# Three branches for the loads of a pass's last two heads, with smaller pieces only for the last pass

## The chip, the cores and the metric

One core of one Trainium2 chip. The time is the device time of one execution in microseconds; lower is better. The kernel before takes 1071.82 us (median of 3 runs, 1071.46 to 1071.98). The trace is one further execution with its own span, some 2 us shorter than the time.

## The reference

Softmax over rows of given scores, times v:

```python
batch, n_heads, seq, head_dim = 8, 12, 1024, 64      # scores: 8 x 12 x 1024 x 1024 fp32, v: 8 x 12 x 1024 x 64 fp32
scores_max = np.max(scores, axis=-1, keepdims=True)
attn = np.exp(scores - scores_max)
attn = attn / (np.sum(attn, axis=-1, keepdims=True) + 1e-8)
return np.matmul(attn, v)
```

There are 96 heads, each with 4 MB of scores, 256 KB of v and 256 KB of output.

## The kernel before

A loop of 24 passes handles four heads each, with one buffer per head for scores and v. A head's 1024 rows lie as 128 partitions x 8 rows ("row" below means one of these 8: 128 x 1024 scores). For each two rows ACT takes the exponential, for each row PE transposes it in eight 128x128 blocks, DVE copies the transposed row out of PSUM, and PE multiplies it with v (two rows later, `LAG`). A column of ones beside v gives the row sums; after four rows DVE divides. When the last row of head k has been transposed, the load of head k of the next pass is issued on SP's queue, which also has the stores.

```python
    def load(k, n, step=R, **cond):                     # R = 8 rows a head, AHEAD = 4 heads a pass
        queue(nc.sync.dma_start(out=v_bufs[k][:], in_=one(v_bh, n), **cond))
        for r in range(0, R, step):
            queue(nc.sync.dma_start(out=s_bufs[k][:, r : r + step, :],
                                    in_=one(sc_bh, n)[:, r : r + step, :], **cond))

    def load_next(k, n0):
        n = (n0 + (AHEAD + k)) % BH
        load(k, n, R if k < AHEAD - 1 else R // 2, cond=n0 < BH - AHEAD)   # skipped in the last pass

    def heads(n0):
        for k in range(AHEAD):
            nc.gpsimd.tensor_copy(out=vones_bufs[k][:, :, 0:D], in_=v_bufs[k][:])
            ...
            for r in range(R):
                if r % EB == 0:                         # EB = 2 rows
                    p_nat = take(p_bufs)
                    nc.scalar.activation(out=p_nat[:], in_=s_bufs[k][:, r : r + EB, :], func=EXP)
                ...                                     # eight transposes of row r into psT
                nc.vector.tensor_copy(out=pt[:], in_=psT[:])
                if r == R - 1:
                    load_next(k, n0)
                pending.append((n0 + k, r, pt, st))
                if len(pending) > LAG:                  # LAG = 2
                    finish(pending.pop(0))              # matmuls with v; after 4 rows divide; after 8 store
        while pending:
            finish(pending.pop(0))

    for k in range(AHEAD):
        load(k, k)
    with tc.For_i(0, BH, AHEAD, iteration_sync="reg_based") as n0:
        queued.clear()
        heads(n0)
```

`queue` keeps the transfers on SP in the order written. The build gives each transfer one of eight completion semaphores in turn, and each transfer waits until the earlier user of its semaphore has landed (in the trace of before the stores wait 292 us in all for loads of scores).

The softmax here doesn't subtract the row's maximum and nothing guards it: scores larger than these inputs give would overflow.

## Time and profile before

| | before |
|---|---|
| time, median of 3 | 1071.82 us |
| span of the trace | 1070.1 us |
| queue in service | 99.7% of the span |
| busiest compute engines (PE, ACT) | 70%, 69% |
| a pass at the queue's rate | 43.9 us |
| last landing of scores | about 1057.1 us |
| last write of out_sb ends | 1066.29 us |

The share of busy time says that data movement bounds the kernel; the timeline of the last pass says what follows the last landing. The prediction below shows the lines of both. A landing is read as the moment at which an engine's idle time before an instruction ends. One more view of before is needed, the busy table of three stretches of the tail (stretch, its length, then busy us and number of instructions of PE, PE's weight loads, DVE, ACT and POOL, the granted tensor clock, the DMA share and GB/s; in such short stretches the last two are rough):

```profile
1044.00:1048.00 4.00, 1.49 (x28) 1.24 (x26) 2.16 (x5) 1.66 (x1) 0.30 (x1) 1.00 1.03 432
1048.00:1052.00 4.00, 3.69 (x47) 3.70 (x48) 1.99 (x5) 4.00 (x4) 0.32 (x1) 0.59 1.04 446
1052.00:1056.00 4.00, 3.72 (x74) 3.60 (x72) 3.13 (x7) 4.00 (x3) 0.00 (x0) 0.98 0.85 351
```

PE has little to do before head 2 lands at 1046.3 (1.49 of 4 us).

### The profile page before, as it was taken

How to read it: one execution, taken by the hardware profiler on the slowest of the kernel's cores; microseconds unless marked ns; L12 is line 12 of the kernel's file. 1: busy time of each engine (PE TensorE's matmuls, PEld its weight loads, DVE VectorE, ACT ScalarE, POOL GpSimd, SP SyncE). 2: the span in 40 equal slices, each digit the busy share in tenths (PEclk: the TensorE clock that was granted, in tenths of full speed). 3: DMA queues.
4: the chain of work that ended last, by engine and by line, in shares of the span. 5: the costliest groups of instructions: out<-in, count | busy, mean ns of one | idle time of the engine just before them, and what ended most of it. 6: DMA issues, size and time to landing. Idle time of an engine off the chain costs nothing.

```text
span 1070.1 us, 31933 instructions
## 1 busy us (share of the span) xinstructions
PE 752.8 (70%) x12288; PEld 711.3 (66%) x12288; DVE 610.7 (57%) x1157; ACT 733.8 (69%) x408; POOL 60.1 (6%) x102
## 2 busy tenths in 40 slices
PE   3766768677676776677766768668676776767766
PEld 3766767577666676576765758567675676666766
DVE  2655656456565565555655656556564565655655
ACT  4767766677667776676856767677666776576865
POOL 0000000000000000000000000000000000000000
PEclk9888888778897888877887888888897788878889
DMA  9999999999999999999999999999999999999995
GB/s 401 430 410 430 430 431 425 432 436 431 431 426 425 434 427 425 431 431 430 433 427 434 420 442 430 421 433 426 429 426 434 432 431 431 429 424 440 430 420 228
DMA packets 44787, 453.05 MB, mean 423 GB/s; under 512 B 4976, under 2 KB 4976, under 8 KB 29552
## 3 DMA queue, kind: packets, MB, share of 16 engines
q1 hardware_dynamic: 44784, 453.00, 99.7%
q8 instruction: 3, 0.05, 0.0%
HBM read 445.64 MB, written 25.17 MB: 440 GB/s over the span
## 4 chain that ended last, share of the span: by engine, by line
DMA 67%; PEld 9%; PE 9%; DVE 5%; ACT 5%; SPq 2%; issue 2%; ACTq 0%
DMA s_nat<-in_scores_dram 67%; PEld L169 7%; PE psT L169 6%; DVE pt L175 5%; ACT p_nat L163 5%; PE psO L105 3%; PEld L105 3%; SPq L140 1%; SPq L143 1%; SPq L124 0%; DVE recip L116 0%; ACTq L163 0%; DVE out_sb L117 0%
## 5 line engine op out<-in xcount | busy, mean ns | idle before, releaser
L163 ACT ACTIVATE p_nat<-s_nat 128x2048 f16<-128x2048 f32 x384 | 703.0, 1902 | 159.2 <-DMA s_nat<-in_scores_dram 157.0
L175 DVE COPY pt<-psT 128x1024 f16<-128x1024 f16 x768 | 516.3, 690 | 432.3 <-PE L169 214.5
L169 PE MATMUL psT<-ident,p_nat 128*128 128x128 f16 x6144 | 569.7, 251 | 267.3 <-ACT p_nat L163 266.6
L169 PEld LDWEIGHTS <-p_nat 128*128 128x128 f16 x6144 | 492.9, 153 | 282.2 <-ACT p_nat L163 277.7
L105 PE MATMUL psO<-vones,pt 128*128 128x65 f16 x6144 | 374.8, 205 | 45.3 <-DVE pt L175 38.9
L105 PEld LDWEIGHTS <-pt 128*128 128x128 f16 x6144 | 305.2, 106 | 71.8 <-DVE pt L175 70.1
L163 ACT ACT_TABLE_LOAD x24 | 30.8, 1283 | 168.1 <-DMA s_nat<-in_scores_dram 163.2
L158 POOL CAST vones<-v_sb 128x512 f16<-128x512 f32 x96 | 59.4, 619 | 987.6 <-DMA v_sb<-in_v_dram 725.0
L117 DVE TENSOR_TENSOR out_sb<-psO,recip 128x256 f32<-128x256 f32 x192 | 81.1, 422 | 4.9
L116 DVE RECIPROCAL recip<-psO 128x4 f32<-128x4 f32 x192 | 33.5, 174 | 17.2 <-PE psO L105 17.2
L57 DVE MEMSET vones<- 128x8 f16 x4 | 0.2, 65 | 0.8 <-PEq L204 0.8
L51 DVE CAST ident<-ident 128x128 f16<-128x128 f32 x1 | 0.2, 226 | 0.3 <-POOL ident masks.py:199 0.3
masks.py:199 POOL TENSOR_SCALAR_AFFINE_SELECT ident<-ident 128x128 f32<-128x128 f32 x1 | 0.3, 294 | 0.1
masks.py:197 POOL MEMSET ident<- 128x128 f32 x1 | 0.2, 205 | 0.3 <-POOLq L204 0.3
L204 POOL MEMSET const-float32-0.0<- 128x1 f32 x1 | 0.1, 99 | 0.2 <-issue 0.2
L204 POOL MEMSET const-bfloat16-1.0<- 128x1 bf16 x1 | 0.1, 102 | 0.0
L204 POOL MEMSET const-uint8-127<- 128x1 uint8 x1 | 0.1, 102 | 0.0
L204 POOL MEMSET const-float32-1.0<- 128x1 f32 x1 | 0.1, 99 | 0.0
## 6 DMA issues: line engine op xcount, KB each, us to landing
s_nat<-in_scores_dram SPq DMA_DIRECT2D x76, 4096.0 KB, 27.1
s_nat<-in_scores_dram SPq DMA_DIRECT2D x48, 2048.0 KB
v_sb<-in_v_dram SPq DMA_DIRECT2D x100, 256.0 KB, 17.2
out_dram<-out_sb SPq DMA_DIRECT2D x96, 256.0 KB, 21.1
```

The lines of the kernel that those rows point to most:

```text
L51: nc.vector.tensor_copy(out=ident16[:], in_=ident32[:])
L57: nc.vector.memset(vo[:, :, D : D + 1], 1.0)
L105: nc.tensor.matmul(out=psO[:, g, :], lhsT=pt[:, c * P : (c + 1) * P], rhs=st["vones"][:, c, :], start=(c == 0), stop=(c == C - 1),)
L116: nc.vector.reciprocal(out=recip[:], in_=psO[:, :, D : D + 1])
L117: nc.vector.tensor_tensor(out=st["out_sb"][:, r - G + 1 : r + 1, :], in0=psO[:, :, 0:D], in1=recip[:].to_broadcast([P, G, D]), op=mybir.Al ...
L140: queue(nc.sync.dma_start(out=v_bufs[k][:], in_=one(v_bh, n), **cond))
L143: nc.sync.dma_start(out=s_bufs[k][:, r : r + step, :], in_=one(sc_bh, n)[:, r : r + step, :], **cond,)
L158: nc.gpsimd.tensor_copy(out=vones_bufs[k][:, :, 0:D], in_=v_bufs[k][:])
L163: nc.scalar.activation(out=p_nat[:], in_=s_bufs[k][:, r : r + EB, :], func=EXP)
L169: nc.tensor.transpose(out=psT[:, c * P : (c + 1) * P], in_=p_row[:, c, :], identity=ident16[:],)
L175: nc.vector.tensor_copy(out=pt[:], in_=psT[:])
L204: nc = _bacc.Bacc("TRN2", target_bir_lowering=False, num_devices=1)
```

## The change

The intent: in the last pass, work should follow closely behind the data, so the last two heads of that pass come in pieces (4,4 rows and 2,2,2,2 rows). In other passes whole heads are loaded. As the loop body is one program for all passes, this choice is a branch at the end of the pass: whole heads; or pieces for the last pass, loaded in the last but one; or nothing, in the last pass itself. Apart from that, the last two rows of each pass's last head get an exponential each.

```diff
-    def load(k, n, step=R, **cond):
+    def load(k, n, parts=(R,), **cond):
 ...
     def load_next(k, n0):
-        n = (n0 + (AHEAD + k)) % BH
-        load(k, n, R if k < AHEAD - 1 else R // 2, cond=n0 < BH - AHEAD)
+        if k < AHEAD - 2:
+            load(k, (n0 + (AHEAD + k)) % BH, cond=n0 < BH - AHEAD)
+
+    def load_last(n0):
+        before = queued[-1:]
+        def loads(parts2, parts3):
+            queued[:] = before
+            load(AHEAD - 2, (n0 + (2 * AHEAD - 2)) % BH, parts2)
+            load(AHEAD - 1, (n0 + (2 * AHEAD - 1)) % BH, parts3)
+        with tc.If(n0 < BH - 2 * AHEAD) as cmp:
+            loads((R,), (R,))
+        with cmp.Else():
+            with tc.If(n0 < BH - AHEAD):
+                loads((4, 4), (2, 2, 2, 2))
 ...
-                    nc.scalar.activation(
-                        out=p_nat[:], in_=s_bufs[k][:, r : r + EB, :], func=EXP
-                    )
+                    rows = 1 if k == AHEAD - 1 and r == R - EB else EB
+                    for g in range(0, EB, rows):
+                        nc.scalar.activation(
+                            out=p_nat[:, g : g + rows, :],
+                            in_=s_bufs[k][:, r + g : r + g + rows, :],
+                            func=EXP,
+                        )
 ...
         while pending:
             finish(pending.pop(0))
+        load_last(n0)
```

More of the change, by code (lines that the diff above doesn't have):

```diff
@@ L137, in apart @@
         )
-    def load(k, n, step=R, **cond):
+    def load(k, n, parts=(R,), **cond):
         queue(nc.sync.dma_start(out=v_bufs[k][:], in_=one(v_bh, n), **cond))
-        for r in range(0, R, step):
+        r = 0
+        for rows in parts:
             queue(
                 nc.sync.dma_start(
-                    out=s_bufs[k][:, r : r + step, :],
-                    in_=one(sc_bh, n)[:, r : r + step, :],
+                    out=s_bufs[k][:, r : r + rows, :],
+                    in_=one(sc_bh, n)[:, r : r + rows, :],
                     **cond,
@@ L148, in load @@
             )
+            r += rows
     def load_next(k, n0):
-        n = (n0 + (AHEAD + k)) % BH
-        load(k, n, R if k < AHEAD - 1 else R // 2, cond=n0 < BH - AHEAD)
+        if k < AHEAD - 2:
[11 more added lines that the diff above has]
+                loads((4, 4), (2, 2, 2, 2))
     def heads(n0):
```

## The prediction

> **What bounds the kernel now.** I read the page first: busy shares, the forty slices, the queues, the chain. Then the waits, and last the timeline of each engine over the first 100 us and the last 70 us, because the change speaks of "the last pass".
>
> The page's engine line, slices, queue share and chain:
>
> ```profile
> PE 752.8 (70%) x12288; PEld 711.3 (66%) x12288; DVE 610.7 (57%) x1157; ACT 733.8 (69%) x408; POOL 60.1 (6%) x102
> DMA  9999999999999999999999999999999999999995
> GB/s 401 430 410 430 430 431 425 432 436 431 431 426 425 434 427 425 431 431 430 433 427 434 420 442 430 421 433 426 429 426 434 432 431 431 429 424 440 430 420 228
> q1 hardware_dynamic: 44784, 453.00, 99.7%
> DMA 67%; PEld 9%; PE 9%; DVE 5%; ACT 5%; SPq 2%; issue 2%; ACTq 0%
> ```
>
> No compute engine is above 70%. The one queue that carries the data was in service for 99.7% of the span, and only the last of the forty slices is not full. So for some 1057 us of 1070 the kernel is its traffic, 453 MB, at about 430 GB/s. A head is 4096 + 256 + 256 KB; a pass of four heads is 18.87 MB, and 18.87 MB / 430 GB/s = 43.9 us.
>
> ACT at the end of the run (start, duration, what, idle before it and what ended that):
>
> ```profile
> 1002.40 14.72 ACT L163 ACTIVATE p_nat<-s_nat 128x2048 f16<-128x2048 f32 x8 [3.65 <-DMA s_nat<-in_scores_dram]
> 1024.41 1.28 ACT L163 ACT_TABLE_LOAD   x1 [7.28 <-DMA s_nat<-in_scores_dram]
> 1025.70 7.32 ACT L163 ACTIVATE p_nat<-s_nat 128x2048 f16<-128x2048 f32 x4
> 1035.41 7.32 ACT L163 ACTIVATE p_nat<-s_nat 128x2048 f16<-128x2048 f32 x4 [2.39 <-DMA s_nat<-in_scores_dram]
> 1046.34 14.71 ACT L163 ACTIVATE p_nat<-s_nat 128x2048 f16<-128x2048 f32 x8 [3.60 <-DMA s_nat<-in_scores_dram]
> ```
>
> Each idle stretch ends with a landing. 1046.34 - 1002.40 = 43.94 us: the pass is the traffic time just worked out. Landings of the last pass: heads 0, 1 and 2 at about 1024.4, 1035.4 and 1046.3. For head 2's eight rows ACT has to wait for the whole head, and from there runs through heads 2 and 3 without a gap.
>
> SP and DVE in the last 45 us:
>
> ```profile
> 1024.48 0.33 SPq L140 DMA_DIRECT2D v_sb<-in_v_dram  x1
> 1025.36 1.19 SPq L143 DMA_DIRECT2D s_nat<-in_scores_dram  x2
> 1035.43 0.36 SPq L124 DMA_DIRECT2D out_dram<-out_sb  x1
> ...
> 1052.51 0.36 SPq L124 DMA_DIRECT2D out_dram<-out_sb  x1
> 1057.35 0.07 SPq L140 DMA_DIRECT2D v_sb<-in_v_dram  x1
> ...
> 1065.87 0.42 DVE L117 TENSOR_TENSOR out_sb<-psO,recip 128x256 f32<-128x256 f32 x1
> 1066.32 0.36 SPq L124 DMA_DIRECT2D out_dram<-out_sb  x1
> ```
>
> In the built program the store at 1052.51 waits for the semaphore of head 3's first half, and the skipped v load at 1057.35 for that of the second half. So these give the last two landings: about 1052.3 and 1057.1. After 1057.1 only 13 us of tail remain: four to five rows of compute still to do, and from the last store's issue to the end 1070.1 - 1066.3 = 3.8 us. ACT started head 3's second half at 1046.34 + 6 x 1.84 = 1057.4, just when it landed: the tail is paced by compute that began at head 2's landing (16 rows), not by the last landing.
>
> [...] the slices here sit at 430, so there is nothing for the steady state to gain. [...] The trace before has a loop branch 24 times and shows no cost above the 43.94 us of traffic; whether the new branches stall, no run shows yet.
>
> **The change part by part.**
>
> 1. *Where the loads stand.* Before, SP's order in a pass is: load 0, store 0, load 1, store 1, load 2, store 2, load 3 in halves, store 3 (loads are for the next pass). After: load 0, store 0, load 1, stores 1, 2, 3, then the branch with loads 2 and 3. So loads 2 and 3 now wait for store 3, that is for head 3's whole compute. Is the queue still fed? Call T the landing of head 3. Before T, load 0 is already issued (its semaphore's earlier user, load 2 of this pass, landed at T - 11). Load 1 waits for head 3's own semaphore, issued at T + 1. Head 3's compute takes about 9.5 us after its landing (head 1: landing 1035.4, last out_sb at 1044.8), so store 3 goes at T + 10, loads 2 and 3 between T + 10 and T + 13. At that time the queue still has load 1 and three stores, full until about T + 22.5. Margin about 10 us; cost on the path 0. Likewise at the pass's end SP waits for stores to land (T + 25), while loads 2 and 3 hold the queue until T + 44.
>
> 2. *Branches.* Two compares on each engine, 24 times. Compute engines have 43.9 - 32 = 12 us of slack a pass, SP 10: hidden, cost 0. Only in the last pass, after the last store, SP additionally walks through the empty arm, waits for eight semaphores in turn, and closes: an estimate of 0.5 us on the end.
>
> 3. *Head 3 whole instead of halves.* 22 passes x 128 = 2816 packets fewer of 44787. Heads in halves land no further apart than whole ones (10.8 against 10.9 and 11.0), so worth 0.
>
> 4. *Order of stores in the tail.* Before, stores 2 and 3 of the next to last pass stand behind loads 2 and (store 3) 3; after, both stand ahead of them. 256 KB is 262144 B / 430 GB/s = 0.6 us each. So head 2 of the last pass lands 1.2 us later, head 3 0.6 us later: last landing 1057.7 instead of 1057.1.
>
> 5. *Pieces in the last pass.* Head 2's first four rows land half a head earlier than the whole: 1047.5 - 4.9 = 1042.6. ACT is free of head 1 at 1035.41 + 7.32 = 1042.7, runs them to 1046.4, and continues with rows 4 to 7 at 1047.5 to 1051.2. Head 3 in four pieces of 1 MB (2.4 us each): about 1050.5, 1052.9, 1055.3, 1057.7. Each piece needs 1.84 us on ACT, less than its 2.4 us of landing, so ACT now keeps up with the landings and the tail starts from the last piece: 1057.7.
>
> 6. *The last two rows one at a time.* One 128x1024 exponential: I take 1.0 us (half of 1.90 plus something for the fixed part). Row 7 ready at 1059.8; without the split it would be 1059.6, but row 6 can go a unit earlier. Costs 24 more ACT instructions a run, some 0.1 us a pass, hidden.
>
> The new end: 1059.8 + transposes 0.7 + DVE copy 0.69 + matmuls 0.45 + reciprocal 0.2 + multiply 0.42, with hand-overs about 0.1 = 1062.4, against 1066.29 (1065.87 + 0.42) before: 3.9 us less. Add 0.5 for the empty arm[...]. Sum: 0 in 23 passes, -3.2 us in the tail. 1071.82 - 3.2 = 1068.6 us.
>
> **The rivals.**
>
> *Queue runs dry.* If loads 2 and 3 came later than T + 22.5, every pass would show a gap. For: they move behind store 3, and the trace shows SP blocked at each pass by a few us. Against: the 10 us margin. If the branch plus its waits ate, say, 12 us, the cost would be 2 us x 23 = 46 us, slower by 4%. The waits for balance at the arm's end stand after the loads, so I hold this at 3%.
>
> [...]
>
> *PE becomes the bound of the tail.* Heads 1 to 3 then come without a pause, and the granted clock was 0.59 between 1048 and 1052 and 0.76 between 1040 and 1044 (busy table by stretches). A row costs PE, DVE about 1.0 us at best, so 16 rows from 1045 end at 1061 plus 1.3 for the last matmuls and evacuation: 1062.3, the same as the landing path. If the clock falls for longer, 1 to 2 us of the gain go: 1070.
>
> *Landing later than thought.* Three stores in a row might disturb the reads: 0.1 us a pass would be 2 us in all. Nothing before speaks for it, as a store now goes among reads at every head at 430 GB/s.
>
> **Range and chances.** Gains are bounded: even an end right at the last landing plus 3 us compute and the store cannot save more than 5.5 us, so 1066.3. Losses without a dry queue reach about +2 us. Range 1065.6 to 1072.4. Faster by over 2% (under 1050.4) would need more bandwidth: 0.01. Slower by over 2% (over 1093.3) needs the dry queue: 0.03. The rest, 0.96, within 2%.
>
> **What would show it.** The DMA row stays at 9 in all slices but the last, the queue share at 99.7% or so. The ACT timeline repeats at 43.9 us; a period of 45 or more proves me wrong in step 1. SP's timeline shows loads 2 and 3 about 10 to 13 us after head 3's landing. In the last pass ACT starts head 2 at about 1042.7, then comes in short groups that wait for landings, and its last instruction is two of 128x1024 at about 1058; the last out_sb ends at about 1062.4 and the end follows 4.3 us later. If PE shows a gapless run from 1044 with a clock well under 0.9, the third rival took part of the gain. If the last store is followed by more than 5 us, the empty arm costs more than I put down.

Cut from it: a term of 0.2 us for the tensor clock. The sum had come to -3.2 us and 1068.6 us; with the terms that stand the gain is 3.9 - 0.5 = 3.4 us. Three things that stand were estimates: that the steady state has nothing to gain; that a later place in SP's program lands later by the bytes ahead of it (the landings of before came in the order of issue, 11.0, 10.9 and 10.8 us apart); and 0.5 us for the empty arm, for which the runs below show 0.7.

## The result

The changed kernel takes 1068.99 us (median of 4 runs, 1068.56 to 1069.59), before in the same rounds 1071.9 us. The ratio is 0.9974 (95% interval 0.9957 to 0.9991). A ratio here is the mean time of one kernel's fast runs over that of the other's fast runs of the same rounds, so it is not quite the ratio of the medians. By the 2% rule the two kernels are the same; the interval leaves a gain of 0.1 to 0.4%. The span of the trace went from 1070.1 to 1066.8 us.

The slices and the queue of the changed kernel:

```profile
DMA  9999999999999999999999999999999999999996
q1 hardware_dynamic: 42048, 453.00, 99.8%
```

Nothing runs dry: the row is at 9 up to the last slice. There are 42048 packets instead of 44784 for the same 453 MB.

ACT in the last pass of the changed kernel:

```profile
1023.54 1.28 ACT L182 ACT_TABLE_LOAD   x1 [2.77 <-DMA s_nat<-in_scores_dram]
...
1034.56 7.33 ACT L182 ACTIVATE p_nat<-s_nat 128x2048 f16<-128x2048 f32 x4 [2.40 <-DMA s_nat<-in_scores_dram]
1042.07 3.72 ACT L182 ACTIVATE p_nat<-s_nat 128x2048 f16<-128x2048 f32 x2 [0.19 <-DMA s_nat<-in_scores_dram]
1046.94 7.39 ACT L182 ACTIVATE p_nat<-s_nat 128x2048 f16<-128x2048 f32 x4 [1.15 <-PE L105]
1054.85 1.91 ACT L182 ACTIVATE p_nat<-s_nat 128x2048 f16<-128x2048 f32 x1 [0.52 <-PE L105]
1057.39 2.01 ACT L182 ACTIVATE p_nat<-s_nat 128x1024 f16<-128x1024 f32 x2 [0.63 <-PE L105]
```

Where before has one block of eight activations from 1046.34, ACT now starts head 2 at 1042.07 with its first four rows, and goes in small groups with short waits. The last three waits are put down to PE. I read them as landings, the last at about 1057.3, because SP goes on at the same moments. In the last pass its skipped loads and its stores still wait for the transfer that had their semaphore before:

```profile
1046.96 0.36 SPq L124 DMA_DIRECT2D out_dram<-out_sb  x1
...
1050.00 0.07 SPq L144 DMA_DIRECT2D s_nat<-in_scores_dram  x1
1052.43 10.22 SPq L124 DMA_DIRECT2D out_dram<-out_sb  x3
```

The waits before these three are put down to loads of scores, and SP has two more such waits, which end at about 1054.8 and 1057.25. From 1050.0 on they end about 2.4 us apart, which is one piece of 1 MB, and ACT's groups at 1054.85 and 1057.39 follow the last two. The runs with other pieces below agree, as ACT's waits move with the pieces.

The last write of out_sb on DVE and the last store on SP, changed kernel:

```profile
1061.87 0.42 DVE L117 TENSOR_TENSOR out_sb<-psO,recip 128x256 f32<-128x256 f32 x1
1062.32 0.33 SPq L124 DMA_DIRECT2D out_dram<-out_sb  x1
```

So out_sb is complete at 1062.29 instead of 1066.29, 4.0 us earlier, and from the last store's issue to the end there are 1066.8 - 1062.3 = 4.5 us instead of 3.8. Together 3.3 us, the whole difference between the two spans.

The tensor clock in the same three stretches, changed kernel:

```profile
1044.00:1048.00 4.00, 3.45 (x68) 3.20 (x66) 3.36 (x7) 2.85 (x2) 0.40 (x1) 1.00 1.02 430
1048.00:1052.00 4.00, 3.50 (x69) 3.25 (x68) 3.11 (x7) 4.00 (x3) 0.21 (x1) 1.00 1.01 426
1052.00:1056.00 4.00, 3.53 (x71) 3.29 (x70) 3.25 (x7) 3.48 (x3) 0.00 (x0) 1.00 0.86 352
```

PE has no pause before head 2 any more and works at a clock of 1.00 all through; it does 69 matmuls between 1048 and 1052 where before did 47.

One ordinary pass of the changed kernel, ACT at the start of head 3 and then SP:

```profile
573.71 7.42 ACT L182 ACTIVATE p_nat<-s_nat 128x2048 f16<-128x2048 f32 x5 [3.07 <-PE psO L105]
```

```profile
575.11 11.07 SPq L124 DMA_DIRECT2D out_dram<-out_sb  x3
586.65 0.35 SPq L140 DMA_DIRECT2D v_sb<-in_v_dram  x1
587.32 0.35 SPq L144 DMA_DIRECT2D s_nat<-in_scores_dram  x1
...
588.76 0.33 SPq L144 DMA_DIRECT2D s_nat<-in_scores_dram  x1
```

With head 3's landing taken as T = 573.7, store 3 is the last of the three stores, issued at 586.18 - 0.35 = 585.8 or T + 12.1; the v load of head 2 goes at T + 12.9, the scores of heads 2 and 3 at T + 13.6 and T + 15.1. From the end of the last store's issue to the v load there are 0.47 us, and between two ordinary issues next to each other 0.32 us, so the branch itself costs SP about 0.15 us.

### The profile page after: what moved, and what is told of

It reads as the page before. It is cut to its first block, busy times and chain, and to the rows that moved or that the text cites. A ratio compares the mean times of both kernels' runs of the same rounds, so it can differ in the third digit from the quotient of the medians.

```text
span 1066.8 us, 32321 instructions
## 1 busy us (share of the span) xinstructions
PE 762.6 (71%) x12288; PEld 722.4 (68%) x12288; DVE 609.8 (57%) x1157; ACT 736.3 (69%) x432; POOL 59.9 (6%) x102
## 2 busy tenths in 40 slices
DMA packets 42051, 453.05 MB, mean 425 GB/s; under 512 B 4672, under 2 KB 4672, under 8 KB 29248
## 3 DMA queue, kind: packets, MB, share of 16 engines
q1 hardware_dynamic: 42048, 453.00, 99.8%
## 4 chain that ended last, share of the span: by engine, by line
DMA 49%; PE 20%; PEld 9%; ACT 8%; DVE 7%; issue 3%; SPq 3%; DVEq 0%; ACTq 0%
DMA s_nat<-in_scores_dram 49%; PE psT L190 13%; ACT p_nat L182 8%; PE psO L105 7%; PEld L190 6%; DVE pt L196 5%; PEld L105 3%; DVE out_sb L117 2%; SPq L140 1%; SPq L124 1%; SPq L144 1%; DVE recip L116 0%; SPq L166 0%; DVEq L196 0%; ACTq L182 0%
## 5 line engine op out<-in xcount | busy, mean ns | idle before, releaser
L182 ACT ACTIVATE p_nat<-s_nat 128x2048 f16<-128x2048 f32 (+1 forms) x408 | 705.5, 1800 | 253.5 <-DMA s_nat<-in_scores_dram 130.6
L190 PE MATMUL psT<-ident,p_nat 128*128 128x128 f16 x6144 | 583.9, 254 | 257.0 <-ACT p_nat L182 256.1
L190 PEld LDWEIGHTS <-p_nat 128*128 128x128 f16 x6144 | 501.3, 154 | 274.9 <-ACT p_nat L182 271.1
L105 PEld LDWEIGHTS <-pt 128*128 128x128 f16 x6144 | 309.0, 107 | 64.0 <-DVE pt L196 60.3
```

The source lines that it names most:

```text
L105: nc.tensor.matmul(out=psO[:, g, :], lhsT=pt[:, c * P : (c + 1) * P], rhs=st["vones"][:, c, :], start=(c == 0), stop=(c == C - 1),)
L182: nc.scalar.activation(out=p_nat[:, g : g + rows, :], in_=s_bufs[k][:, r + g : r + g + rows, :], func=EXP,)
L190: nc.tensor.transpose(out=psT[:, c * P : (c + 1) * P], in_=p_row[:, c, :], identity=ident16[:],)
```

## The experiments

The theory: the gain is made in the last pass alone, by pieces of both heads, and the branches cost nothing while the queue is full. The rivals: the gain comes from the 22 other passes (fewer packets, another order of transfers); one head's pieces are enough; the branches aren't needed; the queue is near to running dry. The results of all twelve kernels were found correct against the reference. The runs were made in three sessions on three chips; each ratio is to before in the same rounds (1071.9 to 1072.0 us in every session).

### Undoing the pieces: both heads, one head

**Both arms whole.** Edit to the changed kernel:

```diff
-                loads((4, 4), (2, 2, 2, 2))
+                loads((R,), (R,))
```

> The change with its branches and its new order, but both arms load heads 2 and 3 whole (no pieces for the last pass). Theory A (the gain is made only in the last pass, by pieces): head 2 lands whole at about 1046.8, head 3 whole at 1057.3; ACT then has 8 rows left, 7.4 us, so the last out_sb ends near 1067.8 and the span is near 1072.3, time near 1074.4, ratio to before about 1.002. Rival B (the gain comes from the passes: fewer packets, another order of loads and stores, 3 us over 22 passes): the time stays near 1069, ratio 0.997.

Measured: 1075.27 us, ratio to before 1.0028 (1.0014 to 1.0042). Span 1073.2.

**Only head 3 in pieces.**

```diff
-                loads((4, 4), (2, 2, 2, 2))
+                loads((R,), (2, 2, 2, 2))
```

> The change, but in its second arm only head 3 is in pieces (2,2,2,2), head 2 whole. Theory A': both splits are needed, since with head 2 whole ACT starts its last 16 rows at 1046.9 and they pace the end as before: last out_sb at about 1066.9, span about 1071.3, time about 1073.4, ratio 1.0012. Rival D (the last head's pieces alone make the gain): time near 1069.

Measured: 1073.38 us, ratio 1.0013 (0.9999 to 1.0027).

**Only head 2 in pieces.**

```diff
-                loads((4, 4), (2, 2, 2, 2))
+                loads((4, 4), (R,))
```

> The change, but in its second arm only head 2 is in pieces (4,4), head 3 whole. Theory A': head 3's eight rows start only at its landing, 1057.3: ACT ends at 1064.8, last out_sb at about 1067.7, span about 1072.2, time about 1074.3, ratio 1.002. Rival E (head 2's pieces alone make the gain, as it paces the end in before): time near 1069 to 1070.

Measured: 1075.97 us, ratio 1.0037 (1.0023 to 1.005).

ACT's last lines in the three runs, in this order:

```profile
1047.02 7.32 ACT L182 ACTIVATE p_nat<-s_nat 128x2048 f16<-128x2048 f32 x4 [5.05 <-DMA s_nat<-in_scores_dram]
1057.29 7.42 ACT L182 ACTIVATE p_nat<-s_nat 128x2048 f16<-128x2048 f32 x5 [2.95 <-DMA s_nat<-in_scores_dram]
```

```profile
1047.40 14.62 ACT L182 ACTIVATE p_nat<-s_nat 128x2048 f16<-128x2048 f32 x9 [5.12 <-DMA s_nat<-in_scores_dram]
```

```profile
1057.62 7.42 ACT L182 ACTIVATE p_nat<-s_nat 128x2048 f16<-128x2048 f32 x5 [6.56 <-DMA s_nat<-in_scores_dram]
```

All that the change does in the passes is in these three kernels too, and they are 4.4 to 7.0 us slower than the change (medians) and no faster than before. So the pieces of the last pass carry the gain, and both heads need them: with head 2 whole, 16 rows run in one block from its landing; with head 3 whole, eight rows stand behind the last landing. One piece without the other is worth at most 1.9 us (1075.27 to 1073.38), both together 6.3 us (1075.27 to 1068.99). The first of the three is 3.3 us slower than before. Loading head 3 whole makes 2.2 us of that (the run "Head 3 whole in before" below); about 1.1 us is left for the new order with its branch.

For the first and the third my estimate was too low, by 0.9 and 1.7 us. What I had left out is probably the tensor clock, though no run isolates it: between 1060 and 1064 it was 0.62 in the first run and 0.50 in the third, after PE's pause, and out_sb was complete 4.7 and 5.1 us after ACT's end instead of the 2.9 that I took over from the changed kernel.

### Without branches: pieces in every pass

Edit to the changed kernel:

```diff
-        if k < AHEAD - 2:
-            load(k, (n0 + (AHEAD + k)) % BH, cond=n0 < BH - AHEAD)
+        parts = ((R,), (R,), (4, 4), (2, 2, 2, 2))[k]
+        load(k, (n0 + (AHEAD + k)) % BH, parts, cond=n0 < BH - AHEAD)
 ...
-        load_last(n0)
```

> No branch at all: the order of before, with head 2 in 4,4 rows and head 3 in 2,2,2,2 in every pass, and the single-row exponentials. Theory A: the tail is as in the change or better (stores 2 and 3 of the pass before stay behind loads, the empty arm at the end is gone: 0.7 us), span about 1066.0, time about 1068, ratio about 0.9965; the passes stay at 43.9 us because eight transfers in flight still hold at least 10 us of data. Rival C (small pieces in every pass cost queue time or let it run dry, which is why the branches are there): pass period over 44.0 us, time over 1070.

Measured: 1071.09 us, ratio 0.9991 (0.9977 to 1.0005). This is what rival C said; my number was 3 us too low. The tail is as short as in the change: the last piece's exponentials start at 1060.30 and out_sb is complete at 1065.20, 4.9 us later in both. But the pass takes 44.07 us instead of 43.9 and pushes the last landing 3 us back. The queue is in service for 100.2% of the span, so it did not run dry; it moved the same bytes more slowly. That pointed at the number of packets: 54723 instead of 42051.

### What a packet costs

Two runs to test that. **Small packets in before**: each head's scores as even rows and odd rows, two transfers in 4 KB packets.

```diff
-        for r in range(0, R, step):
+        for h in range(2):
             queue(nc.sync.dma_start(
-                    out=s_bufs[k][:, r : r + step, :], in_=one(sc_bh, n)[:, r : r + step, :], **cond))
+                    out=s_bufs[k][:, h::2, :], in_=one(sc_bh, n)[:, h::2, :], **cond))
```

> The kernel of before with each head's scores loaded as even rows and odd rows (two transfers of 2 MB in 4 KB packets: 1024 packets a head instead of 128). If a packet costs 3.7 ns on its engine, as the 0.13 us a pass of the run with pieces in every pass says (12672 packets more over 16 engines took 2.9 us more), a pass of four heads costs 224 packets an engine more, 0.83 us: period 44.75 us, over the run some 19 us, and with whole heads at the end some 3 us more: time about 1094, ratio 1.021. Rival (the 0.13 us a pass came from the lanes or the order of stores, not from packets): period 43.9 to 44.1, time about 1075.

Measured: 1099.19 us, ratio 1.0256 (1.0242 to 1.027).

**Head 3 whole in before**, nothing else:

```diff
-        load(k, n, R if k < AHEAD - 1 else R // 2, cond=n0 < BH - AHEAD)
+        load(k, n, R, cond=n0 < BH - AHEAD)
```

> The kernel of before with one edit: head 3 loaded whole in every pass, no branch. Theory P (a packet costs about 5 ns on its engine: periods 43.891, 43.936, 44.066 and 44.97 us at 0, 8, 32 and 224 packets an engine and pass over whole loads): period 43.89 in the first dozen passes, last landing about 1 us earlier than before (1056.2), but head 3's 8 rows then all behind it: last out_sb at about 1068.3, time about 1074. Rival (halving costs the queue nothing, as the prediction held): period 43.94.

Measured: 1074.16 us, ratio 1.0019 (1.0006 to 1.0033), with the last landing at 1056.3 and out_sb complete at 1068.51. All three as expected.

ACT's table load opens each pass after the landing of head 0, so its start is a good clock of the passes. Twelve passes apart, for before, for before with head 3 whole, and for before with small packets:

```profile
101.78 1.28 ACT L163 ACT_TABLE_LOAD   x1 [7.25 <-DMA s_nat<-in_scores_dram]
629.01 1.28 ACT L163 ACT_TABLE_LOAD   x1 [7.26 <-DMA s_nat<-in_scores_dram]
```

```profile
101.61 1.28 ACT L163 ACT_TABLE_LOAD   x1 [3.59 <-DMA s_nat<-in_scores_dram]
628.32 1.28 ACT L163 ACT_TABLE_LOAD   x1 [3.60 <-DMA s_nat<-in_scores_dram]
```

```profile
102.79 1.28 ACT L163 ACT_TABLE_LOAD   x1 [3.90 <-DMA s_nat<-in_scores_dram]
642.42 1.28 ACT L163 ACT_TABLE_LOAD   x1 [3.88 <-DMA s_nat<-in_scores_dram]
```

| kernel | extra packets an engine and pass | a pass, us (difference / 12) | extra ns a packet |
|---|---|---|---|
| whole heads (nine kernels) | 0 | 43.891 to 43.893 | |
| before (head 3 in halves) | 144 / 16 = 9 | 43.936 | 4.9 |
| pieces in every pass | 576 / 16 = 36 | 44.066 | 4.8 |
| even and odd rows | 3648 / 16 = 228 | 44.969 | 4.7 |

The packets are the differences of the queue's counts in the traces, divided by the passes loaded. A further transfer brings its data packets (128, one a partition) and 16 of under 512 B (the pages count 4976 of these in before and 4672 in the change, for 19 transfers fewer); the expectations above counted the 128 alone, hence their 5 ns. The line is straight over a factor of 25: on the full queue a packet costs 4.7 to 4.9 ns on its engine, for scores in packets of 4 to 16 KB. It is not a cost of transfers: the last two rows of the table both have four transfers more in a pass. What the cost consists of, no run here shows. I used 3.7 ns for the small packets from a first reading of the run with pieces, and so missed its time by 5 us.

For the change this means: whole heads in 22 passes save about 0.044 x 22 = 1.0 us. In the one trace of the changed kernel little of it shows, as passes 14 to 22 of that run (counted from 0) took up to 44.0 us (43.925 on average over 21 passes, before 43.935). All seven traces of kernels with whole heads, a branch and a full queue have such late passes, of up to 44.12 us, from pass 14 at the earliest and pass 21 at the latest; over the run they cost 0.1 to 0.9 us. The two kernels with whole heads and no branch in the loop have none (43.88 to 43.91 us while they loop). So the branch, or the order of transfers that comes with it, may not be quite free; no run separates the two, and the cause stays open. The saving also cancels against an order of stores that costs an estimated 0.6 us (256 KB at 430 GB/s) at the last landing. Without the pieces it cannot outweigh a longer tail: with head 3 whole in before, the pass is shorter and the time 2.2 us longer.

### Without branches: the last two passes behind the loop

Edit to before (the single-row exponentials in the last pass too):

```diff
-    with tc.For_i(0, BH, AHEAD, iteration_sync="reg_based") as n0:
+    with tc.For_i(0, BH - 2 * AHEAD, AHEAD, iteration_sync="reg_based") as n0:
         queued.clear()
         heads(n0)
+    queued.clear()
+    heads(BH - 2 * AHEAD)      # loads the last pass in (R,), (R,), (4, 4), (2, 2, 2, 2)
+    heads(BH - AHEAD)          # loads nothing
```

> No branches: the last two passes stand behind the loop as straight code, pieces only in the last pass, order of before. Theory F (the end of the loop waits for every transfer and engine, so the queue runs empty there): heads of the last but one pass are computed only after its last landing, the queue is empty for about 10 us, time about 1078, ratio about 1.006; one slice of the DMA row at 7 or 8. Rival (the loop's end costs nothing, straight code is the better branch): tail as in the change without the empty arm, time about 1067.7, ratio 0.996.

Measured: 1090.17 us, ratio 1.0169 (1.0155 to 1.0183). ACT around the loop's end, and the queue there:

```profile
1013.58 1.28 ACT L172 ACT_TABLE_LOAD   x1 [37.99 <-PEq L229]
```

```profile
1010.00:1015.00 5.00, 0.00 (x0) 0.00 (x0) 0.00 (x0) 1.41 (x2) 1.41 (x3) 0.50 0.11 43
```

The direction was right: ACT, PE and DVE wait 37 to 38 us at the loop's end until everything has landed, and the queue then stands nearly empty (0.11). The size was three times what I put down, as I counted the empty queue alone. Behind that, the eight heads of the last two passes are computed in a row from 1013.6, 64 rows at about 1.07 us, and that, not the queue, sets the end. So here the branches have a use: they keep the last pass inside the loop.

### The single rows

Edit to the changed kernel:

```diff
-                    rows = 1 if k == AHEAD - 1 and r == R - EB else EB
+                    rows = EB
```

> The change without its single-row exponentials: rows 6 and 7 of each pass's last head in one activation again. Theory: after the last piece's landing at 1057.3 both rows are ready at 1059.3 (in the change row 6 at 1058.4, row 7 at 1059.4), so only row 6's transposes and copy shift; last out_sb ends at about 1062.7 instead of 1062.3, time about 1069.4, a difference at the noise. Rival: the split carries 1 us or more: time 1070 or more.

Measured: 1069.32 us, ratio to before 0.9974 (0.9961 to 0.9988), out_sb complete at 1063.17. Its median is 0.3 us above the change's. In its trace out_sb is complete 0.9 us later, of which 0.35 us is a later last pass (head 0's table load at 1023.89 instead of 1023.54), so the single rows are worth about half a microsecond, which the times cannot tell from nothing.

### How near the queue is to running dry

With both arms whole, one more load or all of them were put behind store 3.

```diff
-        if k < AHEAD - 2:
+        if k < AHEAD - 3:       # and load(1, ...) first in the branch; or k < 0 and load(0, ...), load(1, ...)
```

> As the run with branches and whole heads in both arms, but with head 1's load in the branch too, behind store 3. Theory M (margin is what the queue still holds when loads are issued at about 10.5 us after head 3's landing): only load 0 and three stores are left, 12.2 us, against an issue at 11 to 11.5 us plus a latency of up to 2 us, so the period is 43.9 to 45.0 us, say 44.4; time 1075 to 1100. Rival (two heads in the branch were already near the edge): period over 50 us.

> As before, with all four loads in the branch. Theory M: at head 3's landing nothing is queued but stores, loads come 10 us later, a pass takes 10 + 0.6 + 4 x 10.36 + up to 2 us of latency = 53.5 us: time about 1290, the DMA row at 8 all through. Rival (the queue isn't what feeds the pass): period under 50 us.

The latency of up to 2 us in these two was an estimate. In the trace of before the quickest load of 256 KB landed 2.7 us after its issue, and its data take 0.6 us of that at 430 GB/s.

Measured: 1143.66 us, ratio 1.068 (1.0651 to 1.071), with three heads; 1392.79 us, ratio 1.3005 (1.2979 to 1.3032), with four. Passes took 46.9 and 57.4 us on average. Both are longer than I expected, by 2.5 and 4 us, and by the same two terms. First, head 3 takes 12 us from its landing to store 3 in these kernels and in the change, not 9.5. Second, data flows about 2.5 us after an issue: with four heads, the first v load went at 518.06 and head 0's scores landed at 530.96; 4.46 MB at 430 GB/s are 10.36 us of that. With these, four heads make 12.9 + 2.5 + 4 x 10.36 = 56.8 us, measured 57.4. Three heads: the queue held load 0 and three stores, 10.36 + 1.84 = 12.2 us, and new data flows at 12.9 + 2.5 = 15.4, a gap of 3.2 us; measured 46.9 - 43.9 = 3.0.

For the change, the same sum is 15.4 us against about 22.5 us that the queue still holds: two heads in the branch leave 7 us of margin, three are too many. The rival of a dry queue falls for the change, and these runs show what it would have looked like.

### Taking the empty arm off the end

Two versions meant to beat the change. The branch moves ahead of store 3, to the last row's transposes, so that in the last pass SP has walked the empty arm before it issues the last store. The first version also cut the last head into 2,2,2,1,1:

```diff
-                loads((4, 4), (2, 2, 2, 2))
+                loads((4, 4), (2, 2, 2, 1, 1))
 ...
                 if r == R - 1:
                     load_next(k, n0)
+                    if k == AHEAD - 1:
+                        load_last(n0)
 ...
-        load_last(n0)
```

> A version meant to beat the change: the branch with loads 2 and 3 stands ahead of store 3, so that the empty arm of the last pass is walked before the last store is issued, and store 3 stays behind the last loads; the last head of the last pass comes in rows 2,2,2,1,1. Theory: last landing 0.6 us earlier than in the change (1056.7), one row less behind it, end after the last store 3.8 us instead of 4.5: span about 1065.4, time about 1067.5, ratio to before about 0.996. Rival: DVE paces the last rows or waits for the store of the pass before, and nothing is gained: time 1069.

Measured: 1080.54 us, ratio 1.008 (1.0066 to 1.0094), 13 us off. The trace of POOL and PE near the end:

```profile
1057.28 1.18 POOL L175 CAST vones<-v_sb 128x512 f16<-128x512 f32 x2 [31.23 <-DMA s_nat<-in_scores_dram]
1057.95 0.54 PE L105 MATMUL psO<-vones,pt 128*128 128x65 f16 x7 [10.99 <-POOL vones L175]
```

Head 2's v had long landed, but its cast waited 31 us, and PE waited 11 us for the cast. In the built program the second arm has nine transfers for eight semaphores: the last single row uses the one that head 2's v has, and the cast waits for that semaphore's last count. The next run keeps the place of the branch and takes the ninth transfer away:

```diff
-                loads((4, 4), (2, 2, 2, 1, 1))
+                loads((4, 4), (2, 2, 2, 2))
```

> As the version with rows 2,2,2,1,1, but with the change's own pieces 2,2,2,2, so that the second arm has eight transfers for eight semaphores. Theory (the 8.6 us lost there came from the ninth transfer: its semaphore is also that of head 2's v, so the cast of head 2's v waited 31 us for the last piece): the cast no longer waits, last out_sb at about 1061.7, end 3.8 us after the last store's issue: span about 1065.5, time about 1067.6. Rival (the new place of the branch itself costs it): time 1075 or more.

Measured: 1067.97 us, ratio to before 0.9965 (0.9951 to 0.9978). The 8.6 us by which the version with nine transfers was slower than before are gone, and the edit took only that transfer away, so the ninth transfer was their cause. The last store is issued at 1062.63 and the span is 1066.4, so 3.8 us follow it, as in before, instead of 4.5: the empty arm had cost 0.7 us at the end. The runs above agree: with four, five and seven transfers in the second arm instead of eight, 3.8, 4.1 and 4.4 us follow the last store. The earlier landing that I had also expected did not show: the last exponentials start at 1057.10, 0.3 us earlier than in the change, but out_sb is complete at 1062.60, 0.3 us later. By median this is the fastest kernel, 1.0 us under the change, but the two intervals overlap, and the two were not timed in the same rounds.

## Why the prediction was right

The predicted 1068.6 us came out as 1068.99 us. The gain, put down as 3.2 us, is 2.9 us between the medians and 3.3 us between the two spans. The mechanism is the one named, compute that follows the pieces in the last pass; that the number came so near is in part luck. Counted from the start of the last pass (the table load after head 0's landing), out_sb is complete after 38.75 us instead of 41.88, which is 3.1 us, and the empty arm takes 0.7 of them: the tail gives 2.4 us. The other 0.9 us of the spans is a last pass that began earlier (step 4). Step by step:

1. *Where the loads stand.* Cost on the path 0: right, the queue stayed full. The sizes inside were off: loads at T + 13 to T + 15 instead of T + 10 to T + 13, the margin 7 us instead of 10. I read head 3's compute from head 1 of the last pass (9.5 us). In an ordinary pass it takes 12.1 us, with a clock of 0.71 to 0.73 in its first half.
2. *Branches.* Hidden in the passes: right in the main (about 0.15 us on SP, where the waits are longer), but for the late slow passes above, whose cause is open. The empty arm: 0.7 us, put down as 0.5.
3. *Head 3 whole.* The step that was wrong: "worth 0" is about 0.045 us a pass, 1.0 us in all. I had compared single landings, 0.1 us apart, which cannot show an effect of 0.04; the mean over a dozen passes can. The 2816 packets fewer are also off: with the short packets it is 22 x 144 = 3168, and the last pass has 432 more, so the trace shows 2736 fewer. "Nothing for the steady state to gain" falls with this step: slices of about 430 GB/s, single ones of up to 442, are too coarse to show the tenth of a percent that was there.
4. *Order of stores.* Last landing predicted at 1057.7, read at 1057.3. Counted from head 0's landing in the last pass, the last landing came 32.7 us later in before and 33.8 in the change: 1.1 us more, of which an estimated 0.6 are the store (256 KB at 430 GB/s) and about 0.1 the 432 / 16 = 27 more packets an engine. The rest is within what I can read from the neighbours of a landing: between two kernels with whole heads the new order moves the same distance by 0.7 us (32.97 with head 3 whole in before, 33.71 with both arms whole). It was covered because that pass began 0.9 us earlier: 0.7 us of this was there at the third pass already (101.11 against 101.78), where kernels with the same first passes differ by as much (101.1 to 102.1), so it is not a gain that I can claim for the change.
5. *Pieces.* Head 2 started at 1042.07 (predicted 1042.7), head 3's last piece at 1057.39 (1057.7). Right, and the runs with one head's pieces show that both terms are needed.
6. *Single rows.* 2.01 us for two, so 1.0 each, as taken; with a gain too small for the times to show.

Of the rivals, the dry queue did not come. The fourth, landings later than thought by 0.1 us a pass, resembles the late slow passes, which cost 0.7 us in this trace. The third, PE as the bound of the tail, went the other way. I feared that work without a pause would lower the tensor clock. The clock was higher: 1.00 from 1044 on, where before had 0.59 after a pause. With both arms whole PE was busy for 0.30 us of the stretch from 1044 to 1048, with only head 2 in pieces for 0.42 us of that from 1056 to 1060, and in both the next 4 us had a clock of 0.50. So in these traces the low clock stood after a pause; what sets it, no run isolates. My sum had charged 0.2 us for the clock, and it happened not to matter (luck again), as the landing of the last piece paces the end.

## What to carry to other kernels

When the queue is full for the whole run, the time to look at is what lies behind the last landing (here 13 us of 1070): cut the last transfers so that compute follows them, and follow the chain back through every block that starts late, since the last head's pieces alone were worth 1.9 us and those of both heads 6.3. Cut only there, since the full queue paid for each packet in every pass (4.7 to 4.9 ns on its engine; 44.969 us a pass instead of 43.892 with scores in 4 KB packets, 2.4%). Before moving loads to a later place, add up what the queue still holds then against the issue time plus the delay until data flows (about 2.5 us here), and count the transfers in an arm against the semaphores that they share (with nine for eight a cast waited 31 us for a transfer that it does not read).
